# Three float32r products or one plain float32 product: the context's dense work in a two-layer hybrid backbone

## The chip, the cores and the metric

The kernel runs on one core of a Trainium2 chip as one program. The metric is the device time of one execution in microseconds. The engines are TensorE (PE, with its weight loads as PEld), VectorE (DVE), ScalarE (ACT), GpSimd (POOL) and SyncE (SP), which issues the DMAs. Each has a queue that is served in order.

## The reference

Two layers over 256 context tokens and 512 latent tokens of width 1024. In each layer: a modulated RMSNorm, one input projection, three groups of mixers (S5, gated DeltaNet "GDN", RWKV-7), one output projection with a gated residual, then a modulated RMSNorm and a squared-ReLU MLP (1024 to 4096 to 1024) with a gated residual. The context reads only itself; the latents start from the context's final states. After the first layer the context goes through its output projection and MLP; in the second layer only its states are needed, so its input projection there makes 17 blocks of 128 columns in place of 27, and no output.

```python
hc = rmsnorm(ctx, norm_mlp[layer]) * (1.0 + cmods[4]) + cmods[3]
ctx = ctx + cmods[5] * sq_relu_mlp(hc, mlp_w1[layer], mlp_w2[layer])
```

All of it is float32.

## The kernel before, in words

Activations lie feature-major: tiles of 128 features by 256 (context) or 512 (latent) tokens.

**A dense product** (`product`, L290) makes a float32 product of three float32r products: the weight's high part times the activation's high part, the weight's low part times the activation's high part, the weight's high part times the activation's low part. Their matmuls are all recorded at L296. `weight` (L265) loads 128 rows of 512 values into a staging tile `wl` (L271, 256 KB, issued by SP), casts them to the high part `wh` on ScalarE (L272) and subtracts to get the low part `wo` on VectorE or GpSimd (L273): VectorE for the context's products and the modulation, GpSimd for the latents' output projection and MLP. Each of the three tags has three buffers. `split` (L281) does the same to an activation (L284, L285), and `act_norm` (L974) to a normed one (L980, L981). One tile of weights serves four row tiles: 12 matmuls.

**The arena.** Working tiles come from 18 pages of eight units of 256 columns. A page holds plain or rounded (float32r) values; `set_rounded` (L152) converts pages, each with a copy of one column on the new page (`new_page`, L142, L147). Units are handed out in the order of emission, by a rank of when they are likely to be free. `own` lends pages to S5's pieces.

**The order.** The code emits pairs of jobs (one GDN and one RWKV job of two heads each): three pairs for the context, three for the latents, in each layer. `run_jobs` (L1257) emits each pair's preparation before the recurrences of the one before it. After certain pairs a hook emits dense work: `context` (L1206) after the context's last pair of the first layer: modulation, output projection and MLP of the context; `latents` (L1213) after the latents' last pair: the latents' output projection, then, by way of `between` in `back`, the second layer's input projection of the context (`front`), then the latents' MLP. Each piece is emitted with a class of urgency (`prio`), the recurrences first and the dense work near the end, and a scheduler lays out every engine's queue at build time from these classes. So the context's dense work is interleaved with the recurrences of the latents' pairs, and the order on each engine is fixed before the run.

In the MLP (`back`, L1129) a block of 512 hidden values is four `dense` products of eight row tiles; ScalarE takes the ReLU (L1146), VectorE squares it (L1147), `split` makes its parts, and eight products of four row tiles add to the residual (L1156). The output projection (`out_proj`, L1098) loads the mixers' outputs, splits them, and adds to the residual at L1119. Other lines that are named below: L885 is S5's gate, a plain float32 product of two row tiles of 128 x 128 for each half of the columns and each part of the tokens; L1311, L1318 and L1324 are the heads' loads and stores.

Of the kernel before, what the change touches and what calls it, by code (L numbers as in the profile page):

```python
# [11 lines left out]
AF = mybir.ActivationFunctionType  # L12
# [8 lines left out]
T = CT + LT  # L21
# [3 lines left out]
# tags of small shared tiles: columns, buffers  # L25
# [3 lines left out]
# the arena: pages of UNITS units of UNIT columns  # L29
UNIT, UNITS, PAGES = 256, 8, 18  # L30
PLAIN, ROUND, OWN = range(3)
# classes of urgency
CHAIN, LEVEL, READ, PREP, S5, DENSE, FILL = range(7)

# when the next pair of jobs is prepared, by pair: before the rest of the pair, after its first inverses, after
# its second ones, at its end
# [21 lines left out]
# the mixers' outputs in the order of the rows of the output projection: S5, then by pair of heads  # L58
Y_ORDER = (0, 1, 2, 5, 3, 6, 4, 7)
HALVES = (slice(0, 64), slice(64, 128))  # L60
# columns of a group pair's S5 constants: read-out (re, im), drive, direct part, phases
# [3 lines left out]
class Part:  # L65
    """the context or the latents: first token, tokens, modulation's column."""
# [4 lines left out]
    def chunk(self, d, n):  # L71
        """the chunk of step n in direction d."""
        return self.nc - 1 - n if d else n

    def chunks(self, d, n0, n1):
        """the chunks of the steps n0 .. n1 as a slice."""
        if d == 0:
            return slice(n0, n1)
        return slice(self.nc - 1 - n0, self.nc - n1 - 1 if n1 < self.nc else None, -1)
# [10 lines left out]
class Kern:  # L90
# [26 lines left out]
    def prio(self, c):  # L117
        """what is emitted inside is scheduled before the higher classes, in its own order."""
# [16 lines left out]
    def d(self, w):  # L135
        """a short-lived tile of the dense work."""
        return self.tile("s", w)

    # The arena hands out units by the order of emission: they go back at the end of the scope they are
    # taken in, or with release() of the list keep. Each free unit carries a rank of when it is likely to  # L140
    # be free indeed. A page holds plain float32 or float32r values.
# [10 lines left out]
    def set_rounded(self, count):  # L152
        """makes count of the pages hold float32r."""
# [13 lines left out]
    def own(self, count, late, pieces):  # L167
        """lets what the pieces emit take its tiles from count pages of its own; late: jobs that they outlast."""
# [14 lines left out]

    def s(self, w, p=P, keep=None, kind=None):
# [5 lines left out]
        for pg in self.pages:  # L190
            if pg.kind != kind:
                continue
            for o in range(0, UNITS - u + 1):
# [3 lines left out]
                # early free, not beside tiles of another life, not across quarters and halves  # L197
# [36 lines left out]
    def load_layer(self, l):  # L234
# [4 lines left out]
        # derived columns  # L239
# [25 lines left out]
    def weight(self, src, eng):  # L265
        """the parts of 128 rows of up to 512 values; eng: the engines that take turns at the low one."""
# [9 lines left out]
    def rows(self, src, eng):  # L276
        """by row tile the parts of 4 x 128 rows of a block of 128 columns."""
# [12 lines left out]
    def product(self, ps, w, acts, first=True, last=True, fresh=False):  # L290
        """ps += sum over k of w[k].T @ act[k]; fresh: the low parts of acts come last."""
        nc = self.nc
        terms = [[(hi, ah), (lo, ah), (hi, al)] for (hi, lo), (ah, al) in zip(w, acts)]
# [4 lines left out]
    def dense(self, src, acts, n, eng, fresh=False):  # L298
        """out^T[128 cols, tokens] for one block of 128 columns, in psum."""
# [6 lines left out]
    def rows_rstd(self, ps, n, scale, eps, tag):  # L306
        """(ps * scale + eps) ** -0.5 on a small token-major tile."""
# [7 lines left out]
    def bcast(self, r, w, sel, nt, tag, rt):  # L315
        """r [128 tokens, w per tile] back to feature-major, in psum; rt: scratch."""
# [18 lines left out]
    def solve(self, probs, nc_):  # L335
        """probs: pairs of blk, ytt. blk(h): [128, step, direction, 64] whose rows of half h hold strictly
        triangular blocks N on their diagonal; the inverses of I - N replace them. ytt takes the transposes
# [1582 lines left out]
```

## Time and profile before

| what | value |
|---|---|
| median of 3 timed runs | 3077.45 us (3076.12 to 3078.54) |
| span of the profiled execution, first to last instruction | 3056.7 us |
| PE busy | 2669.4 us (87%), 19956 matmul records |
| DVE, ACT, POOL busy | 1833.7, 1186.7, 1134.5 us |
| mean granted TensorE clock | 0.875 |
| DMA | 401.73 MB, 41.6% of 16 engines for the main queue |

The timed executions have no separate figure for the profiled one; its span stands 20.75 us below their median. The page counts an engine as busy from the start to the end of each instruction; matmuls are pipelined, so the distance between two starts is shorter than the time of one. In the chain that ended last the line of the dense products (L296) has 35% of the span.

### The profile page before, as it was taken

What the parts mean: (1) busy time and instruction counts of PE and PEld (TensorE: products, weight loads), DVE (VectorE), ACT (ScalarE), POOL (GpSimd) and SP (SyncE); (2) the same over time, 40 slices, a digit from 0 to 9 for tenths busy, and PEclk for the clock granted to TensorE, in tenths of its full rate; (3) what the DMA queues carried; (4) which work ended last, traced back from release to release, by engine and by line L of the source; (5) the groups of instructions that cost most, each with busy time, mean ns of one, the idle gap of its engine ahead of it and who ended that gap; (6) DMA issues with size and microseconds to landing.
All of it is one profiled execution on the core that took longest, in us unless ns stands there. A gap on an engine that the chain in (4) does not pass through costs nothing.

```text
span 3056.7 us, 54445 instructions
## 1 busy us (share of the span) xinstructions
PE 2669.4 (87%) x19956; PEld 2044.2 (67%) x19956; DVE 1833.7 (60%) x4462; ACT 1186.7 (39%) x2411; POOL 1134.5 (37%) x1274
## 2 busy tenths in 40 slices
PE   5789998865898999987899989889887889799998
PEld 1667776543566888876666768667655567477776
DVE  6654878765667756647876562647776753332223
ACT  2344445332534543445423423353334432133332
POOL 2532335424133121123446644344442522244443
PEclk9788999676787999987999999889987859699998
DMA  5345546543653543535233332255555632022222
GB/s 196 96 140 185 151 136 210 154 130 86 200 161 120 166 157 116 167 114 161 85 88 111 125 96 93 102 187 159 148 184 165 211 93 86 28 83 94 93 94 86
DMA packets 324651, 401.73 MB, mean 131 GB/s; under 512 B 142880, under 2 KB 173472, under 8 KB 324256
## 3 DMA queue, kind: packets, MB, share of 16 engines
q1 hardware_dynamic: 324384, 398.24, 41.6%
q8 instruction: 158, 2.59, 0.4%
q14 instruction: 109, 0.89, 0.1%
HBM read 300.76 MB, written 88.90 MB: 127 GB/s over the span
## 4 chain that ended last, share of the span: by engine, by line
PE 53%; DVE 19%; DMA 9%; issue 5%; ACT 4%; SPq 3%; POOL 1%; DVEq 0%; ACTq 0%; POOLq 0%
PE d L296 35%; DMA page<-dr 3%; DVE solve L371 3%; DVE solve L373 3%; PE rc L1733 2%; DVE wo L273 2%; PE rc L1732 2%; PE p L1622 1%; DVE s L472 1%; DMA dr<-page 1%; SPq L352 1%; DMA s<-s 1%; DMA wl<-in_w_dram 1%; ACT wh L272 1%; PE p L481 1%
## 5 line engine op out<-in xcount | busy, mean ns | idle before, releaser
L296 PE MATMUL d<-page,wh 128*128 128x512 f32 (+1 forms) x5024 | 1424.8, 367 | 61.0 <-DVE page L1156 15.5
L296 PEld LDWEIGHTS d<-page,wh 128*128 128x128 f32 x5024 | 919.0, 196 | 234.5 <-DVE page L1156 18.0
L296 PE MATMUL d<-page,wo 128*128 128x512 f32 (+1 forms) x2512 | 915.2, 365 | 5.5 <-DVE wo L273 4.3
L272 ACT CAST wh<-wl 128x512 fp32r<-128x512 f32 (+1 forms) x750 | 457.1, 616 | 710.2 <-PE d L296 421.0
L273 POOL TENSOR_TENSOR wo<-wl,wh 128x512 fp32r<-128x512 f32 (+1 forms) x357 | 471.8, 1325 | 672.0 <-ACT wh L272 635.8
L296 PEld LDWEIGHTS d<-page,wo 128*128 128x128 f32 x2512 | 493.4, 196 | 80.6 <-DVE wo L273 5.8
L273 DVE TENSOR_TENSOR wo<-wl,wh 128x512 fp32r<-128x512 f32 (+1 forms) x393 | 296.1, 758 | 112.6 <-ACT wh L272 104.1
L1156 DVE SCALAR_TENSOR_TENSOR page<-d,mod,page 128x512 f32<-128x512 f32 (+1 forms) x192 | 124.8, 659 | 199.6 <-PE d L296 199.1
L371 DVE TENSOR_TENSOR solve<-solve 128x30 f32<-128x30 f32 (+4 forms) x360 | 151.3, 420 | 21.6 <-issue 12.0
L1147 DVE TENSOR_TENSOR s<-s 128x512 f32<-128x512 f32 (+1 forms) x96 | 60.5, 631 | 172.1 <-ACT s L1146 172.0
L373 DVE TENSOR_TENSOR solve<-solve 128x30 f32<-128x30 f32 (+4 forms) x360 | 142.8, 397 | 7.7
L1499 POOL TENSOR_TENSOR g<-g,gates 64x128 f32<-64x128 f32 x120 | 59.5, 496 | 219.7 <-DVE g L1504 190.4
L285 DVE TENSOR_TENSOR page<-s,page 128x512 fp32r<-128x512 f32 (+1 forms) x118 | 86.6, 738 | 47.5 <-ACT page L284 47.3
L1146 ACT ACTIVATE s<-d 128x512 f32<-128x512 f32 (+1 forms) x96 | 50.6, 527 | 141.5 <-PE d L296 141.4
L472 DVE SCALAR_TENSOR_TENSOR s<-s,ncol,s 128x256 f32<-128x256 f32 (+1 forms) x132 | 96.4, 733 | 3.0
L284 ACT CAST page<-s 128x512 fp32r<-128x512 f32 (+1 forms) x118 | 64.1, 547 | 80.5 <-DVE s L1147 62.9
L926 PE MATMUL d<-wo,scp 128*2 128x512 f32 x160 | 76.3, 477 | 20.6 <-DVE wo L273 19.6
L1622 PE MATMUL p<-page,page 64*128 64x128 f32 (+1 forms) x576 | 84.7, 307 | 10.4 <-DVE page L1625 7.1
L1622 PEld LDWEIGHTS p<-page,page 64*128 64x128 f32 x576 | 73.1, 209 | 27.4 <-issue 12.8
L1733 PE MATMUL rc<-page,page 128*64 128x64 f32 x464 | 86.7, 275 | 2.8 <-DMA page<-dr 2.8
L481 PE MATMUL p<-consts,page 128*128 128x128 f32 x348 | 63.8, 309 | 25.0 <-DMA page<-dr 11.2
L1732 PE MATMUL rc<-page,r 64*64 64x64 f32 x432 | 79.2, 270 | 5.6 <-DVE r L1724 4.0
(464 smaller groups left out, 4057.7 us busy)
## 6 DMA issues: line engine op xcount, KB each, us to landing
wl<-in_w_dram SPq DMA_DIRECT2D x384, 256.0 KB, 2.6
wl<-in_mod_w_dram SPq DMA_DIRECT2D x160, 256.0 KB, 3.0
wl<-in_w_in_dram SPq DMA_DIRECT2D x142, 256.0 KB, 2.9
page<-dr SPq DMA_DIRECT2D x118, 256.0 KB, 3.3
dr<-s SPq DMA_DIRECT2D x72, 256.0 KB, 2.5
dr<-page SPq DMA_DIRECT2D x30, 512.0 KB, 4.1
dr<-page SPq DMA_DIRECT2D x55, 256.0 KB, 2.5
page<-dr SPq DMA_DIRECT2D x16, 834.0 KB, 5.2
```

The costliest lines, as they stand in the source:

```text
L272: nc.scalar.copy(hi, st)
L273: low.tensor_tensor(lo, st, hi.bitcast(F32), OP.subtract)
L285: nc.vector.tensor_tensor(lo, src, hi.bitcast(F32), OP.subtract)
L296: nc.tensor.matmul(ps, x, y, start=(first and i == 0), stop=(last and i == len(order) - 1))
L371: nc.vector.tensor_tensor(tm, y3[:, :j, j:j + 1].to_broadcast([P, j, w]), y3[:, j:j + 1, j + 1:].to_broadcast([P, j, w]), OP.mult)
L373: nc.vector.tensor_tensor(y3[:, :j, j + 1:], y3[:, :j, j + 1:], tm, OP.add)
L472: nc.vector.scalar_tensor_tensor(acc, cp[:, j:j + n], w[:, 5 * i + j:5 * i + j + 1], acc, OP.mult, OP.add)
L481: self.nc.tensor.transpose(p[:, t * 128:(t + 1) * 128], src[:, t * 128:(t + 1) * 128], self.ident)
L1156: nc.vector.scalar_tensor_tensor(x[j], ps, mod[:, 40 + j, g:g + 1], x[j], OP.mult, OP.add)
L1622: nc.tensor.matmul(ps[:, i], flat(bk[d][hs, n0 + i]), kr[d][hs, n0 + i], start=True, stop=True)
L1732: nc.tensor.matmul(o, st[hs, d], kr[d][hs, n, 1], start=True, stop=False)
L1733: nc.tensor.matmul(o, xv[h][:, n, d], self.R[d][:, h, n], start=False, stop=True)
```

## The change

The context's output projection, its MLP and its input projection of the second layer call the same helpers with no split engine (`eng` is None). `rows` then loads the weights into `wl` and hands them to the matmul as they are; the activations are plain float32 tiles too, taken from pages that `held` sets aside (three for output projection and MLP, one for the input projection). `product` makes one matmul call for each row tile. The conversion to four rounded pages ahead of the context's dense work goes away; the latents' conversion to six stays. The small second products of the decay and learning rate (`lora`) keep their splits on VectorE. The rest of the diff takes out comments.

```diff
-PLAIN, ROUND, OWN = range(3)
+PLAIN, ROUND, OWN, HELD = range(4)
...
+    @contextmanager
+    def held(self, count):
+        free = sorted((p for p in self.pages if p.kind == PLAIN and None not in p.rank), key=lambda p: max(p.rank))[:count]
+        assert len(free) == count
+        for p in free:
+            p.kind = HELD
+        yield
+        for p in free:
+            p.kind, p.rank = PLAIN, [max(max(p.rank), self.now + 0.5)] * UNITS
...
     def rows(self, src, eng):
+        if eng is None:
+            st = self.wide("wl")
+            self.nc.sync.dma_start(st, src.rearrange("p k n -> p (k n)"))
+            st = st.rearrange("p (k n) -> p k n", k=4)
+            return [st[:, k] for k in range(4)]
...
     def product(self, ps, w, acts, first=True, last=True, fresh=False):
         nc = self.nc
+        if not isinstance(w[0], tuple):
+            for i, (x, y) in enumerate(zip(w, acts)):
+                nc.tensor.matmul(ps, x, y, start=(first and i == 0), stop=(last and i == len(w) - 1))
+            return
...
-    def act_norm(self, x, part, gain, mod, sh, rs=None):
+    def act_norm(self, x, part, gain, mod, sh, rs=None, plain=False):
         nc, acts = self.nc, []
         for k, h in enumerate(self.norm(x, part, gain, mod, sh, rs)):
+            if plain:
+                t = self.s(part.n, kind=HELD)
+                nc.scalar.activation(t, h, AF.Identity, bias=mod[:, sh + k, part.g:part.g + 1])
+                acts.append(t)
+                continue
...
-        eng = 'p' if part is LAT else 'v'
+        eng = 'p' if part is LAT else None
...
-                    t = self.d(n)
+                    t = self.s(n, kind=HELD) if eng is None else self.d(n)
                     nc.sync.dma_start(t, self.yd[l, part][k])
-                    b = self.new_act(n)
-                    self.split(b, t)
+                    if eng is None:
+                        b = t
+                    else:
+                        b = self.new_act(n)
+                        self.split(b, t)
...
-                            r = self.d(n)
+                            r = self.s(n, kind=HELD) if eng is None else self.d(n)
                             nc.scalar.activation(r, ps, AF.Relu)
                             nc.vector.tensor_tensor(r, r, r, OP.mult)
+                            if eng is None:
+                                us.append(r)
+                                continue
                             b = self.new_act(n)
                             self.split(b, r)
...
         def context():
-            self.set_rounded(4)
             mods(1, 0, 2, 1, 3)
             xc[:] = self.load_x(xin(CTX), CTX, kc)
-            self.out_proj(0, CTX, xc, (0, 1))
-            self.back(0, CTX, xc, lambda: mods(0, *range(4 + 6, 12)))
+            with self.held(3):
+                self.out_proj(0, CTX, xc, (0, 1))
+                self.back(0, CTX, xc, lambda: mods(0, *range(4 + 6, 12)))
...
-            self.back(0, LAT, xl, lambda: self.front(1, ((CTX, xc, kc),), 'v'))
+            def front1():
+                with self.held(1):
+                    self.front(1, ((CTX, xc, kc),), None)
+            self.back(0, LAT, xl, front1)
```

## Rows read from the trace of the kernel before

**Rows 1.** Busy time by stretch: from:to, us; PE, PEld, DVE, ACT, POOL (instructions); clock, DMA share, GB/s.
```profile
814.00:940.00 126.00, 111.39 (x1036) 78.57 (x1035) 87.87 (x215) 51.33 (x108) 37.11 (x43) 0.78 0.50 152
940.00:1215.00 275.00, 262.27 (x3112) 229.80 (x3113) 185.78 (x457) 122.22 (x257) 53.01 (x69) 0.95 0.46 143
1215.00:1281.00 66.00, 58.64 (x441) 55.40 (x440) 53.52 (x180) 33.99 (x69) 5.76 (x5) 0.95 0.56 183
...
1325.00:1430.00 105.00, 84.94 (x564) 74.88 (x564) 66.89 (x157) 59.49 (x141) 29.65 (x55) 0.84 0.49 151
...
1470.00:1920.00 450.00, 420.01 (x2587) 324.23 (x2587) 271.33 (x603) 158.91 (x312) 231.27 (x232) 0.97 0.34 104
```

**Rows 2.** The same stretches, instructions of L296 alone: PE, PEld, clock, DMA share, GB/s.
```profile
814.00:940.00 126.00, 29.99 (x192) 26.40 (x192) 0.78 0.50 152
940.00:1215.00 275.00, 157.94 (x1120) 142.22 (x1121) 0.95 0.46 143
1215.00:1281.00 66.00, 56.52 (x425) 53.77 (x424) 0.95 0.56 183
...
1325.00:1430.00 105.00, 60.25 (x408) 56.42 (x408) 0.84 0.49 151
```

**Rows 3.** Groups by shape, 814 to 1430: count, busy us, mean ns, idle before and releasers.
```profile
L296 PE MATMUL d<-page,wh 128*128 128x256 f32 x1424 | 291.3, 298 | 16.6 <-DVE page L1156 4.1 <-DVE page L981 3.8 <-ACT page L980 3.3
...
L296 PE MATMUL d<-page,wo 128*128 128x256 f32 x712 | 210.7, 296 | 3.8 <-DVE wo L273 3.8
L273 DVE TENSOR_TENSOR wo<-wl,wh 128x512 fp32r<-128x512 f32 x196 | 140.2, 720 | 46.1 <-ACT wh L272 43.8 <-PE d L926 0.2
L272 ACT CAST wh<-wl 128x512 fp32r<-128x512 f32 x215 | 131.9, 618 | 195.1 <-PE d L296 132.6 <-DMA wl<-in_w_out_dram 17.9 <-DMA wl<-in_w_dram 15.1
```

**Rows 4.** Waits of ACT, 940 to 1281: us in total, times, longest.
```profile
ACT wh L272 <- PE d L296: 77.2, 45, 5.2
```

**Rows 5.** Waits of PE, 940 to 1281.
```profile
PE d L296 <- DVE page L981: 2.8, 1, 2.8
...
PE d L296 <- DVE page L285: 2.1, 1, 2.1
PE d L296 <- DVE wo L273: 1.4, 2, 1.1
...
PE d L296 <- ACT wh L272: 1.2, 2, 0.9
```

**Rows 6.** Busy time by stretch, columns as in rows 1: two short stretches for clock.
```profile
747.30:749.40 2.10, 2.10 (x7) 0.94 (x5) 2.10 (x3) 1.02 (x3) 0.23 (x1) 1.00 0.00 0
1242.30:1245.20 2.90, 2.90 (x27) 2.90 (x26) 2.86 (x13) 1.27 (x3) 0.00 (x0) 1.00 0.51 143
```

**Rows 7.** Timeline of PE in the context's MLP: start us, us, instruction, count.
```profile
1243.09 0.40 PE L296 MATMUL d<-page,wh 128*128 128x256 f32 x2
1243.32 0.28 PE L296 MATMUL d<-page,wo 128*128 128x256 f32 x1
1243.44 0.40 PE L296 MATMUL d<-page,wh 128*128 128x256 f32 x2
```

**Rows 8.** Timeline of PE in S5's gate.
```profile
747.28 0.59 PE L885 MATMUL d<-page,page 128*128 128x256 f32 x2
747.72 1.02 PE L885 MATMUL d<-page 128*128 128x512 f32 x2
748.58 1.02 PE L885 MATMUL d<-page,page 128*128 128x512 f32 x2
```

**Rows 9.** Line L885 in the whole trace: count, ns min/median/max, first and last start.
```profile
L885 PE MATMUL d<-page,page x24: 379/613/1220, 743.7 to 2359.9; 128*128 128x256 f32 x12, 128*128 128x512 f32 x12
...
L885 PE MATMUL d<-page x8: 379/592/667, 730.5 to 748.1; 128*128 128x256 f32 x4, 128*128 128x512 f32 x4
```

**Rows 10.** Waits of SP's queue, 940 to 1281.
```profile
SPq L271 <- DVE wo L273: 116.8, 59, 14.4
```

**Rows 11.** Weight tiles (wl), 900 to 1430, from issue to landing.
```profile
DMA to landing us min/median/max: 2.2/2.8/5.6
```

More of the change, by code (lines that the diff above doesn't have):

```diff
@@ L1000, in front @@
             for part, x, kept, *rs in parts:
-                acts.append(self.act_norm(x, part, col["norm_mix"], mod, 0, *rs))
+                acts.append(self.act_norm(x, part, col["norm_mix"], mod, 0, *rs, plain=eng is None))
                 self.release(kept)
@@ L1061, in lora @@
                         nc.vector.tensor_tensor(y[HALVES[1 - d], :n], x[hs], y[hs, :n].bitcast(F32), OP.subtract)
-                        hi, lo = self.weight(a["ups"][l, i, d], eng)
+                        hi, lo = self.weight(a["ups"][l, i, d], eng or "v")
                         for f in range(3):
@@ L1132, in back @@
         col, mod = self.par[l]
-        eng = 'p' if part is LAT else 'v'
+        eng = 'p' if part is LAT else None
         with self.prio(DENSE):
@@ L1137, in back @@
             with self.scope():
-                acts = self.act_norm(x, part, col["norm_mlp"], mod, 24)
+                acts = self.act_norm(x, part, col["norm_mlp"], mod, 24, plain=eng is None)
                 for fb in range(8):
```

## The prediction, made before any run of the changed kernel

> **What bounds the kernel now.** I read the busy time of each engine by stretch first, because the change touches three stretches only: the context's output projection (814 to 940 us, with modulation products in it), the context's MLP (940 to 1281) and the second input projection of the context (1325 to 1430). In 940 to 1281 TensorE is busy 262.27 + 58.64 = 321 of 341 us, VectorE 239, ScalarE 156 [rows 1]. The reader is to see that TensorE has 20 us left there, VectorE 102. In the first and the third stretch TensorE has 15 and 20 us left [rows 1].
>
> The same windows for the line of the dense products alone give 157.94 + 56.52 = 214 us of TensorE in 940 to 1281, so the heads' work takes 107 there; in the third stretch 60 of 85 [rows 2]. The groups by shape show what is replaced: 1424 + 712 = 2136 products of 256 columns, and beside them the splits of weights: 196 on VectorE of 0.720 us, 215 casts of 0.618 us on ScalarE (both counts hold some of other weights) [rows 3].
>
> Then the waits. ScalarE's cast of a weight stands 77.2 us, 45 times, behind TensorE [rows 4]: the high and low parts have three buffers each and TensorE has not read the old ones. TensorE in turn waits 2.8 + 2.1 + 1.4 + 1.2 = 7.5 us for splits of activations and weights [rows 5]. So weights are ready before TensorE wants them. In the context's MLP the dense work is bound by TensorE, not by what the change takes away.
>
> **The price of a product.** At the full clock (the clock column reads 1.00, the level of 2.4 GHz, for both stretches that I use [rows 6]) three split products start 1243.44 - 1243.09 = 0.35 us apart in all, 0.117 each [rows 7]. The plain product exists in this kernel too, in the gate of S5 (L885). Two of its records of 256 columns take 747.72 - 747.28 = 0.44 us, two of 512 columns 748.58 - 747.72 = 0.86 [rows 8]. So one record of 256 columns is 0.215 us, which looks like a bargain against 0.35. But the code there makes 2 layers x 2 halves x 2 parts x 2 row tiles = 16 products, and the trace holds 24 + 8 = 32 records [rows 9]. Each plain product is two records: 0.43 us against 0.35 for the three. The change makes the dense work 0.08 us dearer for each 128 rows by 256 columns: 64 products in the output projection (+5 us), 512 in the MLP (+41), 136 in the input projection (+11), 57 us in all.
>
> TensorE's weight loads are the place to weigh a rule. In 940 to 1215 they are busy 229.80 of 275 us [rows 1], yet the steps of 0.117 us [rows 7] show that they overlap. The Trainium skill (Perfetto Trace Analysis, Identifying the Most-Contended Engine) calls the busy share of matmuls a bad measure and that of LDWEIGHTS a good one. By that rule the change would relieve TensorE, since 2136 loads become 1424; by the measured starts it burdens it. I go by the starts; the other result is the last rival.
>
> **The change part by part.** The sum is made on the profiled execution (span 3056.7); the timed runs' median is 20.75 us above that span, and I add the difference in the span to the median.
>
> Output projection (814 to 940): +5 us of TensorE beside 15 idle ones [rows 1], so nothing of it need reach the end; if that cover is gone it costs the 5. Sixteen weight tiles lose their cast and split, and eight loaded outputs theirs. The heads' recurrence of the first latent pair runs through the same stretch and does not change. Bounds: nothing, and 16 x 0.720 = 11.5 us [rows 3] if every VectorE split were on the path. I take 7 gained, since the products queue behind VectorE's triangular solve as well, which stays.
>
> MLP (940 to 1281): +41 on the engine that bounds it. Back come the 7.5 us of waits for splits [rows 5]. The bare steps of 1545 records are 1545 x 0.117 = 181 us against 214 busy [rows 2]; about 10 of the 33 us between are the mean clock of 0.95 [rows 1], and of the remaining 23 (last passes and short gaps) I give back half, 12, since a square feeds the product without cast and split, and ScalarE's queue no longer stands behind TensorE. 41 - 7.5 - 12 = 21 later. Bounds: TensorE's floor, 107 + 512 x 0.43 = 327, which would be 14 earlier; and the full 41 later.
>
> Input projection (1325 to 1430): +11 of TensorE, 20 idle, 36 splits on VectorE less. This stretch also waits for transfers, shifts and convolutions. Bounds -12 (the idle time filled, the +11 paid out of it, and the start of the norm a little earlier) and +11; I take +2, near the middle.
>
> Transfers: the same count and bytes. What moves is the wait: SP's issue of a weight now stands mostly on VectorE's split (116.8 us, 59 times) [rows 10]; afterwards on TensorE's last product of the tile three before. Queued behind it on SP are the heads' loads and stores, and their recurrences wait for those. A transfer lands in 2.2 to 5.6 us, 2.8 in the middle [rows 11]; two tiles of four products, 3.44 us, cover the middle one and not the longest. I count it as nothing, as the middle says; the rival below has its price.
>
> Pages: three set aside in place of four that hold rounded values, one page more for the heads; the conversion of four pages goes away before the output projection, and at the latents six are converted in place of two. Each is a copy of one column on VectorE that waits for the page's last reader, with VectorE's queue behind it. Counted as nothing: VectorE has 102 us free. If that cover fails, a wait like the longest of an in-order engine on these products, 5.2 us [rows 4], is the bound for one, either way.
>
> What follows starts with the end of these stretches. The latents' MLP (1470 to 1920) keeps TensorE busy 420 of 450 us [rows 1] and is not edited, so a delay passes through whole. Sum: -7 + 21 + 2 = +16, so 3077.45 + 16 = **3093 us**.
>
> **Rivals.**
> - **TensorE is filled to its floor** (faster). VectorE loses some 92 us of splits in 940 to 1281 (128 tiles of 0.720 us [rows 3]); the heads' steps, which queue behind them, come sooner and leave no gaps. For it: only 107 of the 341 us are the heads' TensorE work. Against it: TensorE is at 321 of 341. The place is 940 to 1281, and it decides when over 20 of the 41 us are regained there. Its time: -14 - 12 - 12 = -38, 3039.
> - **Three buffers are too few** (slower still). A weight tile is held till TensorE is through, not till it is split, so the lead over TensorE shrinks from weights and parts, six deep, to three. It decides where a landing takes over 3.44 us. At the longest, 5.6, a tile's turn is (5.6 + 1.72) / 3 = 2.44 us, 0.72 over its 1.72; if a third of the 178 tiles land so, 59 x 0.72 = 43 more: 3136. For it: the DMA share is 0.46 to 0.56 already [rows 1], and SP serves all in order. Against it: the middle landing of 2.8 us.
> - **Nothing reaches the end**: regained waits and dearer products cancel, 3077.
> - **Weight loads bound TensorE**: 712 loads fewer at a step of 0.117 us each [rows 7] are 83 us, 2994. The starts of plain records [rows 8] speak against it, though only a few stand in a row in this trace.
>
> **How the numbers follow.** A measurement of this kernel can tell about 0.2% (6 us) from no change. Forecast case 0.46 (its own range +0 to +36: 0.39 slower, 0.07 within 6 us); floor rival 0.26, faster; three buffers 0.16, slower; nothing 0.08 (0.05 same, 0.02 faster, 0.01 slower); loads 0.04, faster. Faster 0.32, same 0.12, slower 0.56. Those on the slower side hold 0.55 with a range of their own of 3083 to 3138; the whole range, with the upper half of the floor rival in, is 3042 to 3138.
>
> **What would show it.** Right: in the context's MLP the records of the dense line number 1024 at 0.215 us and its stretch is some 20 us longer, with TensorE over 94% busy; no casts of weights there; SP's longest waits are on TensorE; the output projection's stretch a few us shorter. Wrong: one record for each product; a context MLP that ends before 1281; TensorE idle for long before the dense line, released by transfers of weights (then it is the buffers); or a first latent pair that starts elsewhere than near 814, since the order of all engines is laid out anew at build time.

## The result, and the profile after

The changed kernel takes 3149.32 us (median of 4 runs, 3146.77 to 3152.09) against 3076.78 for the kernel before beside it: a ratio of 1.0253, 95% interval 1.0223 to 1.0283. It is slower by 72 us where the prediction had 16. The profiled execution took 3152.09 us, its span is 3150.1.

In the changed kernel the plain products are recorded at L312, the split ones at L317 (L296 before); plain weight tiles are issued at L291 and split ones at L282 (L271 before), L1175 and L1188 are the ReLU and the residual's sum (L1146, L1156 before).

Busy time by stretch of the changed kernel, columns as in [rows 1]: output projection, MLP, second input projection.

```profile
830.00:955.00 125.00, 111.52 (x1047) 77.39 (x1047) 78.08 (x201) 41.77 (x91) 41.08 (x49) 0.82 0.46 136
955.00:1330.00 375.00, 362.04 (x3036) 285.15 (x3036) 135.17 (x361) 69.92 (x160) 47.16 (x67) 0.96 0.44 137
1375.00:1490.00 115.00, 96.45 (x433) 76.03 (x434) 45.33 (x121) 43.62 (x111) 27.13 (x56) 0.83 0.49 151
```

The same stretches for L312 alone, columns as in [rows 2].

```profile
830.00:955.00 125.00, 33.97 (x128) 24.96 (x128) 0.82 0.46 136
955.00:1330.00 375.00, 242.76 (x1024) 190.64 (x1024) 0.96 0.44 137
1375.00:1490.00 115.00, 71.41 (x272) 56.55 (x272) 0.83 0.49 151
```

The count settles the price's first half: 128 + 1024 + 272 = 1424 records for 712 products, two each. Beside [rows 1], the MLP's stretch grew from 341 to 375 us, TensorE in it from 321 to 362, while VectorE fell from 239 to 135 and ScalarE from 156 to 70. TensorE has 13 us left where it had 20.

The timeline of PE there shows the other half, as [rows 7] did for the split steps: 13 records from 1199.69 to the next instruction at 1202.59, 0.223 us each, 0.45 a product. The third line has the busy time of that stretch, columns as in [rows 1]; its clock column reads 1.00, as it did for the two prices of the prediction.

```profile
1199.69 2.97 PE L312 MATMUL d<-page,wl 128*128 128x256 f32 x13
1202.59 0.45 PE L1548 MATMUL gc<-page,g 128*64 128x64 f32 x8
...
1199.70:1202.50 2.80, 2.80 (x14) 2.28 (x12) 1.48 (x4) 0.38 (x1) 0.00 (x0) 1.00 0.03 7
```

Waits in 955 to 1330 of PE and SP, and the landing of weight tiles in 900 to 1490 (columns as in [rows 5], [rows 10] and [rows 11]).

```profile
PE d L312 <- DMA wl<-in_w_dram: 4.1, 5, 2.0
...
SPq L291 <- PE d L312: 211.2, 106, 7.0
...
DMA to landing us min/median/max: 2.4/2.7/6.4
```

TensorE's waits for splits [rows 5] are gone, and 4.1 us of waits for transfers have come. SP waits on TensorE as foretold, 211 us in all, and by these rows it hardly matters: a weight is late five times. Whether more staging tiles would gain anything, e3 below has to tell.

A row of SP gives the length of a piece between its first and its last weight transfer, which I use from here on where nothing else is said. The first line is the context's MLP of the kernel before (profile on which the prediction rests), the second that of the changed kernel, the third the changed kernel's second input projection (columns: count; min/median/max ns; first and last start).

```profile
L271 SPq DMA_DIRECT2D wl<-in_w_dram x128: 327/328/1350, 915.0 to 1272.0; - x128
```

```profile
L291 SPq DMA_DIRECT2D wl<-in_w_dram x128: 327/328/1191, 931.1 to 1323.6; - x128
...
L291 SPq DMA_DIRECT2D wl<-in_w_in_dram x34: 327/330/859, 1362.3 to 1475.2; - x34
```

The MLP went from 357.0 to 392.5 us, the projection from 102 to 113. This length has a weakness: the first transfer goes out ahead of the first product, and not by the same time in every kernel. The products of the MLP themselves, in the kernel before, in the changed one and in e4 (an experiment below):

```profile
L296 PE MATMUL d<-page,wh x1024: 276/279/681, 943.7 to 1279.0; 128*128 128x256 f32 x171
```

```profile
L312 PE MATMUL d<-page,wl x1024: 379/379/796, 968.2 to 1328.4; 128*128 128x256 f32 x171
```

```profile
L301 PE MATMUL d<-page,wl x1024: 379/379/795, 937.4 to 1312.7; 128*128 128x256 f32 x171
```

From the first to the last of them it is 335 us before, 360 in the change and 375 in e4: 25 and 40 us more, where the transfers say 36 for both. So the size of the MLP's part depends on the measure, by up to 15 us between the two kernels.

The rest of the 72 us lies outside the three parts. Transfers of weights read from SP's queue (the first of a piece where nothing else is said), and the end of the span, in us (e0 is the kernel before run again; e4, e13 and e15 are experiments below):

| | output projection | MLP of the context | latents' MLP, 10th tile | latents' MLP, last | second layer's MLP | end |
|---|---|---|---|---|---|---|
| before, e0 | 823 | 925 | 1483 | 1918 | 2657 | 3062 |
| changed | 830 | 931 | 1553 | 1987 | 2747 | 3150 |
| e4 | 817 | 915 | 1507 | 1946 | 2690 | 3094 |
| e13 | 824 | 921 | 1527 | 1959 | 2689 | 3094 |
| e15 | 822 | 923 | 1505 | 1944 | 2688 | 3092 |

The output projection starts 7 us late in the changed kernel, before a plain product has run; the latents' MLP gets going late; and the second layer, where nothing was edited, loses another 20 us.

### The profile page after: what moved, and what is told of

It reads as the page before. It is cut to its first block, busy times and chain, and to the rows that moved or that the text cites. A ratio compares the mean times of both kernels' runs of the same rounds, so it can differ in the third digit from the quotient of the medians.

```text
span 3150.1 us, 52340 instructions
## 1 busy us (share of the span) xinstructions
PE 2755.5 (87%) x19244; PEld 2058.0 (65%) x19244; DVE 1713.9 (54%) x4227; ACT 1070.4 (34%) x2193; POOL 1134.2 (36%) x1275
## 5 line engine op out<-in xcount | busy, mean ns | idle before, releaser
L317 PE MATMUL d<-page,wh 128*128 128x512 f32 (+1 forms) x3600 | 1133.1, 394 | 46.3 <-DVE page L1188 12.8
L317 PEld LDWEIGHTS d<-page,wh 128*128 128x128 f32 x3600 | 683.0, 195 | 206.2 <-DVE page L1188 16.0
L317 PE MATMUL d<-page,wo 128*128 128x512 f32 (+1 forms) x1800 | 705.6, 392 | 3.3 <-POOL wo L284 3.0
L283 ACT CAST wh<-wl 128x512 fp32r<-128x512 f32 (+1 forms) x572 | 348.1, 616 | 608.4 <-PE d L317 329.5
L317 PEld LDWEIGHTS d<-page,wo 128*128 128x128 f32 x1800 | 351.1, 195 | 74.5 <-POOL wo L284 5.9
L312 PE MATMUL d<-page,wl 128*128 128x256 f32 x1424 | 348.1, 398 | 9.0 <-DMA wl<-in_w_dram 4.1
L312 PEld LDWEIGHTS d<-page,wl 128*128 128x128 f32 x1424 | 272.2, 197 | 59.0 <-issue 6.0
L1188 DVE SCALAR_TENSOR_TENSOR page<-d,mod,page 128x512 f32<-128x512 f32 (+1 forms) x192 | 125.3, 660 | 257.8 <-PE d L317 172.9
L284 DVE TENSOR_TENSOR wo<-wl,wh 128x512 fp32r<-128x512 f32 (+1 forms) x214 | 166.7, 790 | 108.7 <-ACT wh L283 98.4
L301 DVE TENSOR_TENSOR page<-s,page 128x512 fp32r<-128x512 f32 x78 | 71.7, 921 | 45.8 <-ACT page L300 45.6
L946 PE MATMUL d<-wh,scp 128*4 128x512 f32 x160 | 80.4, 503 | 12.9 <-ACT wh L283 10.8
```

The lines of the kernel that those rows point to most:

```text
L283: nc.scalar.copy(hi, st)
L284: low.tensor_tensor(lo, st, hi.bitcast(F32), OP.subtract)
L312: nc.tensor.matmul(ps, x, y, start=(first and i == 0), stop=(last and i == len(w) - 1))
L317: nc.tensor.matmul(ps, x, y, start=(first and i == 0), stop=(last and i == len(order) - 1))
L946: nc.tensor.matmul(ps[:4], self.scp[:, k], hi, start=(k == 0), stop=False)
L1188: nc.vector.scalar_tensor_tensor(x[j], ps, mod[:, 40 + j, g:g + 1], x[j], OP.mult, OP.add)
```

## The experiments

Three theories. **Price**: two records for three steps, and little regained. **Buffers**: three staging tiles are too few. **Pages and order**: other pages, and an order laid out anew at build time, delay work that the change doesn't edit. Ratios are to the kernel before in the same batch; its medians there were 3060 to 3063 us.

### Each part alone, and more staging tiles

e0 is the kernel before again. e1 has only the projection plain, e2 only output projection and MLP:

```diff
# e1: out_proj, back; the context keeps set_rounded(4)
-        eng = 'p' if part is LAT else None
+        eng = 'p' if part is LAT else 'v'
# e2: latents
-                with self.held(1):
-                    self.front(1, ((CTX, xc, kc),), None)
+                self.front(1, ((CTX, xc, kc),), 'v')
# e3: in held, three more staging tiles in the pages set aside
+        mine = []
+        self.turn6, self.extra = 0, [self.s(512, keep=mine, kind=HELD) for _ in range(3)]
...
-            st = self.wide("wl")
+            self.turn6 += 1
+            st = self.wide("wl") if self.turn6 % 2 else self.extra[self.turn6 // 2 % 3]
...
-            with self.held(3):
+            with self.held(4):
...
-                with self.held(1):
+                with self.held(2):
```

> The kernel before once more, for a second profile beside the first, whose span (3056.7 us) stands 20 us below the median of the timed runs. If the 24 us by which the changed kernel's unedited stretches are longer than in the first profile are the spread between executions, this profile shows most of them too (span 3070 to 3077). If they come from the change (the order on the engines, laid out anew), its unedited stretches agree with the first profile within 2 us each.

> Plain products in the context's second input projection alone, the rest as before. The theory of the price (two records of 0.215 us in place of three steps of 0.117, 136 products, little regained) says +8 to +15 us on the kernel before. The theory of the new order (the layout costs, wherever it is touched) says up to +30. The theory of the buffers (three staging tiles held till TensorE is through) says more than the price, since this stretch has the most other transfers: +15 to +25.

> Plain products in the context's output projection and MLP alone, the second input projection with splits as before. Price: 576 products, +46 us at most, some 8 regained: +35 to +45. Buffers: the same here, and it must fall with more staging tiles. Order: with the projection alone the two differ from the full change by more than 15 us in sum.

> The changed kernel with six staging tiles for the plain weights in place of three (three more from one more page set aside). Price: within 8 us of the changed kernel, because SP's wait on TensorE only moves. Buffers: 20 us or more come back, and TensorE's waits for transfers of weights in the context's MLP (4.1 us in sum by the profile) and the gaps before its dense products vanish.

e0: 0.9998 (0.9971 to 1.0025). e1: 3153.74 us, 1.0301 (1.0267 to 1.0335): the cheapest part alone, 136 products, costs as much as the whole change, though its own stretch grows by 7 to 8 us (1313 to 1423) and the last tile of the latents' MLP is issued at 1920, as in e0 (1918). e2: 3126.97, 1.0209 (1.0172 to 1.0246). The parts don't add up, so the price is not all of it. e3: 3183.93, 1.0393 (1.0362 to 1.0424), slower than the change. From its first to its last weight transfer its MLP is no shorter than with three staging tiles:

```profile
L295 SPq DMA_DIRECT2D page<-in_w_dram x64: 327/328/916, 872.3 to 1268.3; - x64
```

That is 396.0 us against 392.5. But with six tiles the first transfers go out earlier, so this length can't tell here, and e3 sets other pages aside than the change. The kernel to hold it against is e11 (below), with the same numbers of pages set aside and three staging tiles. The plain products of output projection and MLP, from e3 (two of its groups), then from e11:

```profile
L316 PE MATMUL d<-page,wl x576: 379/379/796, 834.4 to 1278.3; 128*128 128x256 f32 x192
L316 PE MATMUL d<-page,page x480: 379/379/793, 838.0 to 1280.5; 128*128 128x256 f32 x160
```

```profile
L312 PE MATMUL d<-page,wl x1152: 379/379/796, 834.7 to 1300.0; 128*128 128x256 f32 x192
```

They take 446 us in e3 and 465 in e11 (469 to 471 in e12, e15 and e16, which set four pages aside too and have three staging tiles). For the same two pieces, from the first product of the output projection to the last of the MLP, the kernel before takes 447 (832.1 to 1279.0) and the change 488 (840.8 to 1328.4). So in this stretch six staging tiles are worth some 19 us. At the end little of it is left: e3 at 1.0393 and e11 at 1.0430 are not told apart, since their intervals overlap. Buffers are not the 72 us, but that they cost nothing isn't shown. In e1 and e3 a new thing appears: the preparation of pair 9 (the second layer's first latent pair) is cut in two with over 200 us between, and its triangular solution starts at 2318 and 2339 in place of 2108.

### The price, with the pages of the kernel before

```diff
# e4 on the kernel before (e5: the same in front alone)
+        if eng is None:
...
+            return [st[:, k] for k in range(4)]
...
+                nc.tensor.matmul(ps, x, y.bitcast(F32), start=(first and i == 0), stop=(last and i == len(w) - 1))
...
+            if plain:
+                nc.scalar.activation(hi, h, AF.Identity, bias=shift)
+                acts.append((hi, lo))
+                continue
...
```

> All three parts as plain products, as in the change, but with the pages of the kernel before: every activation keeps its pair of float32r units, takes the value in the high one (rounded to it, so the low parts of these activations are left out of the result), and the plain product reads that unit as float32; the weights stay in their staging tile. What a page holds when is then what it was before, while the order of each engine is again laid out at build time. Price alone (two records of 0.215 us for three of 0.117): the context's MLP, 357 us from its first to its last weight transfer before, takes 357 + 41 - 7 = 391, the second input projection 103 + 5 to 10, and nothing else changes: 3063 + 40 to 50 = 3103 to 3113 us, and the last MLP's first weight transfer at 2657 + 45 = about 2700. Pages (the pages moved by the change cost some 35 to 40 of its 72 us): the same numbers, so the whole time falls from 3149 to 3103 to 3113. Order (the sequence laid out at build time, and not the pages, delays the last pairs): 3140 or more although the context's part comes out at +45, with pair 9's solution after 2200 instead of at 2110.

> Only the second input projection plain, as in the earlier run that took 3154 us, but with its activations in the pairs of units of the kernel before (high part alone, so the low parts of its activations are left out). Pages: the preparation of pair 9 isn't cut in two, the last MLP's first weight transfer stays near 2657, and the whole is 3063 + 0 to 10 = 3063 to 3073 us. Order: 3130 or more, with pair 9's solution again near 2300.

e4: 3099.68, 1.0123 (1.0099 to 1.0146). e5: 3070.96, 1.0038 (1.0018 to 1.0057). In the pages of before the change costs 38 us, not 72 to 77, and the projection 9.5, not 91. e4's MLP:

```profile
L281 SPq DMA_DIRECT2D wl<-in_w_dram x128: 327/328/753, 915.2 to 1307.9; - x128
```

392.7 us, as in the changed kernel and 36 more than before; its output projection takes 98 us to the MLP's start where the kernel before takes 101, its input projection 107 (1346.6 to 1453.6) where the kernel before takes 102. The end is 32 us behind e0 in the two profiles, after a start 5 us ahead: here the context's delay passes through, as I had counted (e13 and e15 will show that it need not).

### Relief and price apart

```diff
# e6 on the kernel before, weights of the three parts
...
+            self.nc.scalar.copy(hi, st)
+            hi = hi.rearrange("p (k n) -> p k n", k=4)
+            return [(hi[:, k], hi[:, k]) for k in range(4)]
# e7 on the changed kernel
+            hi, lo = self.wide("wh", F32R), self.wide("wo", F32R)
+            self.nc.scalar.copy(hi, st)
+            self.nc.vector.tensor_tensor(lo, st, hi.bitcast(F32), OP.subtract)
# e10 on the kernel before, in out_proj, back and front
-        eng = 'p' if part is LAT else 'v'
+        eng = 'p' if part is LAT else 'vp'
```

> The kernel before with its three split steps, but for the weights of the three parts VectorE's subtraction is left out and the high part stands in for the low one (so the low parts of these weights are left out of the result): VectorE's relief without the price, in the pages of before. My prediction gave the MLP 7.5 to 12 us for it: 357 - 12 = 345 us between its first and last weight transfer. If the relief is worth what the change's own stretch shows (41 of price, 34 lost): 350. If nothing waits for VectorE: 357. The whole between 3045 and 3063 us, if the order laid out anew moves nothing.

> The changed kernel, but the casts and subtractions of the weights are still made, into tiles that nothing reads: the price without the relief, in the pages of the change. If the relief is worth 7 us in the MLP: 393 + 7 = 400 us between its first and last weight transfer and 3149 + 10 = 3159. If nothing waited for VectorE and ScalarE once TensorE is slower: 393 and 3149. If the relief was worth more than I read (12 and 7.5, both taken): 393 + 20 = 413 and 3169 or more.

> The kernel before, exact, with the low parts of these three parts' weights taken in turns by VectorE (0.69 us each) and GpSimd (1.30 us each, busy for 65 of the 357 us of the context's MLP): half of the relief without the price of plain products. If the relief is what bound the kernel there: half of the 32 us that leaving out all these subtractions gave, 3061 - 16 = 3045 us, MLP at about 349. If GpSimd's longer subtraction holds TensorE as VectorE's did: 3061 and 357 or slightly longer.

e6: 3029.80, 0.9899 (0.9873 to 0.9926). e7: 3138.13, 1.0252 (1.0221 to 1.0283), the change's own ratio. The MLP of e6, then of e7:

```profile
L279 SPq DMA_DIRECT2D wl<-in_w_dram x128: 327/328/1306, 923.6 to 1263.9; - x128
```

```profile
L291 SPq DMA_DIRECT2D wl<-in_w_dram x128: 327/328/1936, 930.7 to 1312.7; - x128
```

With split products, VectorE's relief takes the MLP from 354 to 357 down to 340, and the whole down by 32. That the whole falls is clear of the spread; where is less sure, since from first to last product e6's MLP takes 324 us, and e8 (below), which makes every subtraction, 325. With plain products the relief is worth nothing that shows: e7 makes every cast and subtraction, its MLP is at 382.0 no longer than without, and its input projection at 118.7 is 6 us longer. Its engines there, columns as in [rows 1], with VectorE at 228 us:

```profile
931.00:1313.00 382.00, 358.55 (x3051) 283.37 (x3050) 228.01 (x507) 149.85 (x301) 63.45 (x77) 0.96 0.42 137
```

The two effects are not a sum. e10: 3067.44, 1.0008 (0.9982 to 1.0033), MLP 932.8 to 1292.4: no gain from half of the relief; the last section has what stands against it.

### Which pages

e8 and e9 take other float32r pages in the kernel before (three; the second to the fifth). The others vary the pages of kernels with plain products:

```diff
# e8 (e9: gone = free[1:5] there)
         def context():
-            self.set_rounded(4)
+            self.set_rounded(3)
# e13 on the changed kernel (e15: with held(4) too; e14: e4 with the projection's activations of the change)
-            if plain:
+            if plain and sh == 0:
+                t = self.new_act(part.n)
+                nc.scalar.activation(t[0], h, AF.Identity, bias=mod[:, sh + k, part.g:part.g + 1])
...
+                y = y[0].bitcast(F32) if isinstance(y, list) else y
# e16 on the changed kernel (e12: the first edit alone; e11: held(4) and held(2))
-            with self.held(3):
+            with self.held(4):
...
-                t = self.s(part.n, kind=HELD)
+                t = self.s(part.n, kind=HELD if sh else None)
...
-                with self.held(1):
-                    self.front(1, ((CTX, xc, kc),), None)
+                self.front(1, ((CTX, xc, kc),), None)
# e17 on the changed kernel, in held
+        free = free[3:4] if count == 1 else free[:count]
```

> The kernel before with three instead of four float32r pages for the context's output projection and MLP: the same instructions but for the marking of a page, the same prices, other pages for the tiles around, and an order laid out anew. Pages/order: it moves the time by tens of us although no work changes, up or down; the place is where a milestone first leaves the kernel before by over 10 us while the lengths of the context's MLP (357 us) and of the second input projection (103 us) stay within 5. If pages and order are harmless, as the prediction counted them: 3061 within 10 us, each milestone within 10.

> The kernel before with four float32r pages for the context as before, but the second to the fifth of the free ones in the order of their ranks instead of the first to the fourth: nothing else differs in the program's text. Pages/order: over 15 us away from 3061, either way. Harmless: 3051 to 3071 us.

> The changed kernel with four and two pages set aside instead of three and one, as in the run with six staging tiles, but with the three staging tiles of the change. If the staging tiles cost nothing there and all of that run's difference was its pages: the same as it, 3180 within 15 us, with the context's MLP again starting near 872 and lasting about 396 us. If the staging tiles mattered: the MLP lasts some 10 us longer than its 396, or starts later. If the change's own choice of three and one is as good as any: 3149.

> The changed kernel with four pages set aside for the context instead of three, one for the second input projection as in the change. If three pages are the cause of the late start of the latents' MLP (10th weight transfer at 1553 in the change, 1502 with four and two pages): about 1505 there. Whether the last pairs follow isn't given by that: 3100 to 3115 if pair 9's preparation runs in one piece, 3180 to 3200 if it is cut in two as with four and two.

> The changed kernel, but the second input projection's plain products read the high units of float32r pairs, as in e4 (the low parts of these activations left out): only the context's three pages are those of the change. If these three carry the cost: as the change, 3140 to 3155. If the projection's page does: as e4, 3100. Both in part, as the run with the output projection and MLP alone has it (3127, without the projection's price of about 5): 3130.

> As e4 (all plain, output projection and MLP in the pages of the kernel before, high parts alone), but the second input projection's activations in one page set aside, as in the change. If that page cuts pair 9's preparation in two whatever stands before it: 3100 + 80 to 90 = 3180 to 3190 with pair 9's solution 200 us later than the preparation's start. If the cut was chance of one layout: 3100 to 3120.

> The changed kernel with four pages set aside for the context, the same four that the kernel before makes float32r, and the projection's activations in the high units of float32r pairs: plain products at the price alone. If the choice of pages is all that the change loses beyond the price: 3100 to 3110 us, as e4. If the six pages that the latents then have to mark anew cost something: 3115 or more, from the latents' MLP on.

> The changed kernel, exact, with four pages set aside for the context's output projection and MLP and none for the second input projection, whose activations take any free float32 units. By the allocation as the kernel is built, no tile of pair 9's preparation falls on a page of the second layer's S5. Page mechanism: pair 9's preparation runs in one piece, and the time is that of the price alone, 3095 to 3115 us. If plain products in exact float32 pages cost more than the price for another reason: 3140 or more.

> The changed kernel, but the one page set aside for the second input projection is the fourth of the free ones in the order of their ranks instead of the first. By the allocation as the kernel is built, a tile of four units of pair 9's RWKV preparation then falls on a page of the second layer's S5, which it doesn't in the change. Page mechanism: pair 9's preparation is cut in two, its solution comes after 2300 us, and the time is 3175 to 3200 us against the change's 3149. If the allocation foretells nothing: 3149 within 10.

e8: 3075.26, 1.0033 (1.0014 to 1.0051), a little slower, by nothing but pages and the order that goes with them. e9: 3070.47, 1.0018 (0.9995 to 1.0041), not told apart from no change. With everything plain, us, by what the projection's activations lie in (rows) and the pages of the context's output projection and MLP (columns):

| | four float32r | three set aside | four set aside |
|---|---|---|---|
| float32r units | 3100 (e4) | 3099 (e13) | 3099 (e15) |
| free units, none set aside | | | 3098 (e16, no low parts left out) |
| one page, the first free | 3188 (e14) | 3149 (the change) | 3180 (e12) |
| one page, the fourth free | | 3205 (e17) | |
| two pages | | | 3196 (e11) |

(The change ran beside a kernel before of 3077 us, the others beside 3060 to 3063; by its ratio it would stand at 3139 here. The ratios of e11 to e15 are 1.0430, 1.0388, 1.0130, 1.0416 and 1.0124, each good to 0.5% or better.) The context's pages make no difference to the whole while the projection's activations lie in float32r units, three medians within 1 us; with four set aside, the projection's page costs 3180 - 3098 = 82. For e13 I had 3130 as the middle case; the three pages carry nothing by themselves. Yet e2, the same three pages with a split projection, is 36 us above what e4 leaves without the projection's price (3127 against 3100 - 9.5), so pages don't add up either.

The first row holds a second lesson. The MLPs of e4, e13 and e15 take 393, 395 and 382 us, and e13 issues the 10th weight tile of the latents' MLP some 21 us after e15 (table above). By the second layer's MLP the three are within 2 us of each other, and they end alike. So a later context isn't always a later end; what makes up for it in the second layer, these runs don't show.

Why one page costs so much can be followed. `own` gives S5 of the second layer the five free pages of the lowest ranks; a page set aside for the projection displaces the tiles that lay there, S5 gets other pages, and then nothing early is free for a tile of pair 9's RWKV preparation (`xv`, the values by step). Printed while the kernels are built, e17's allocation has this line (time of emission, page, units, rank), and the change's has none of rank 20.6 for that pair:

```
now 17.50 page 11 u 4 rank 20.60 prep:1637
```

Rank 20.6 is that of S5's pages. Of the kernels here, e1, e3, e11, e12, e14 and e17 have such a line: 3154, 3184, 3196, 3180, 3188 and 3205 us. None of the others has one. e16 and e17 were foretold from it and came out at 3097.58 (1.0110, 1.0072 to 1.0148) and 3204.95 (1.0461, 1.0420 to 1.0501), the second 5 us over the range that I had given it.

The trace shows it happen. The four copies into the two `xv` tiles of pair 9 on ScalarE, in e16 and then in e17 (columns as for SP above; under e17's what ended the idle time before them):

```profile
L1631 ACT COPY page<-p x4: 364/368/370, 2095.7 to 2096.9; 64x256 f32<-64x256 f32 x4
```

```profile
L1633 ACT COPY page<-p x4: 365/368/370, 2121.1 to 2339.3; 64x256 f32<-64x256 f32 x4
...
  PE d L907: 0.6, 1
```

e17's timeline of ACT and POOL: L907 and L908 are S5's gate (L885 in the kernel before and the line behind it), L910 its last step.

```profile
2337.86 0.47 ACT L908 ACTIVATE page<-d,ncol 128x256 f32<-128x256 f32 x1 [0.18 <-PE d L907]
2338.90 0.76 ACT L1633 COPY page<-p 64x256 f32<-64x256 f32 x2 [0.56 <-PE d L907]
```

```profile
2338.76 2.14 POOL L910 TENSOR_SCALAR page<-page 128x768 f32<-128x768 f32 x1 [5.67 <-DVE page L909]
2340.87 1.93 POOL L1634 TENSOR_SCALAR page<-page 64x512 f32<-64x512 f32 x1
```

The second tile's copies stand from 2121 to 2338 behind the products of S5's gate. In the other five kernels with such a line the same copies lie 214 to 226 us apart, and under 3 us in all kernels without one. The products of that preparation (L1658 in e16, L1660 in e17) show the cut: PE busy, clock, DMA share, GB/s, in four stretches.

```profile
2080.00:2130.00 50.00, 1.42 (x8) 0.93 0.49 156
2130.00:2150.00 20.00, 3.47 (x24) 1.00 0.40 134
2150.00:2340.00 190.00, 0.00 (x0) 0.82 0.47 155
2340.00:2360.00 20.00, 5.21 (x32) 0.83 0.65 197
```

So pair 9's solution, whose first step on VectorE is at 2139.7 in e16, comes at 2371.2 in e17:

```profile
L394 DVE TENSOR_TENSOR solve<-solve x60: 190/358/1801, 2139.7 to 2385.7; 128x30 f32<-128x30 f32 x4, 128x58 f32<-128x58 f32 x4, 128x84 f32<-128x84 f32 x4, 128x108 f32<-128x108 f32 x4
```

```profile
L395 DVE TENSOR_TENSOR solve<-solve x30: 190/386/1408, 2371.2 to 2439.1; 128x30 f32<-128x30 f32 x2, 128x58 f32<-128x58 f32 x2, 128x84 f32<-128x84 f32 x2, 128x108 f32<-128x108 f32 x2
```

How much of e17's 107 us is this wait, and how much the clock that goes with it, isn't separated: the mean granted clock is 0.857 in e17 and 0.876 in e16, and in 2350 to 2600 it is 0.64 and 0.74, with TensorE busy for 194 and 220 of the 250 us.

In the changed kernel itself pair 9's preparation runs in one piece (solution at 2184), and its page costs some 38 us against e13 by the ratios in another way, spread over the run. By the two profiles: 9 by the end of the projection, 26 by the 10th weight tile of the latents' MLP, 40 by the end of the second layer's input projection, 58 by its MLP. These two profiles come from different batches, whose kernels before differ by 17 us, and their mean granted clocks are 0.870 and 0.879, so they show where time is lost rather than how much. No single wait holds it, and how much is the page, how much the order laid out with it and how much the clock stays open. No kernel here that leaves nothing out beats the one before; of those with plain products in all three parts e16 is the fastest.

## Why the prediction was wrong

**The bound, and the price of a product: right.** TensorE bounds the context's MLP, a plain product is two records, and the price fell where it was put. The rival of the weight loads falls: 512 loads fewer in the MLP, and its products take 25 to 40 us longer. The rival of the three buffers had 43 us on top of the forecast; weights are late by 4.1 us in all, and six staging tiles shorten output projection and MLP by 19 us (e3 against e11) without a faster end that can be told from none. So it isn't the cause of the 72 us; the transfers, which I counted as nothing, hold some 19 us of that stretch. The ratio of e4 means 38 us for the whole price where the sum had 16.

**The MLP's term was mis-sized.** I took 41 - 7.5 - 12 = 21. It measured 392.7 - 357.0 = 36 in e4 and the same in the change by the transfers, so 5 to 6 us came back of 19.5; by the products it is 40 in e4 and 25 in the change. Over all the kernels here the plain MLP takes 379 to 396 us by the transfers and the split one 352 to 360, so this size is good to some 10 us. The step that failed is giving back what VectorE and ScalarE no longer do as if it stood beside the price. That relief exists (e6: 32 us in all, 14 to 17 in the MLP by the transfers), but only while split products need the splits; with plain products even the full load of idle casts and subtractions costs nothing that shows (e7).

**The two smaller terms**: output projection -3 in e4 for my -7; input projection 107 for 102 us, +5 for my +2 (the splits that this term counts as 36 are 34, one for each weight transfer; the sum doesn't use them). With the MLP's 15 these make up the 22 us between 16 and 38.

**Pages counted as nothing: wrong, and by the largest amount.** The change's ratio less e4's is 1.30%, 40 us. My bound of 5.2 us was the longest wait of an in-order engine on a matmul; the wait that a page can make is that of a tile for a reader in another job, 217 us in e17. The changed kernel has no such wait: that its 40 us come with the projection's page is shown by e13, by what steps is not. VectorE's 102 us of free time, which I named as the cover, are no cover for a tile that must not be written yet.

**A delay passes through whole**: it does in e4 against e0, and it doesn't in e13 against e15, where 21 us at the latents' MLP are gone by the second layer's. So this step was a guess that e4 bears out and not a rule. The start of the first latent pair was named as the sign of a moved order; the output projection that runs beside it started 7 us later than in e0, but a rerun of the kernel before moves by as much (814 and 823), so this sign was too weak to read.

## What to carry to other kernels

Price a replaced product by the records that the trace has for one product, and give back a neighbour's freed time only if an experiment with the new bound in place shows it: two kernels, one with the relief alone and one with the price and idle work, tell it. Where tiles are placed at build time, a change of placement is an edit like any other: print the allocation, look for tiles that land on a page whose reader is a whole job away, and run the new instructions in the old places before the time is put down to the instructions. Where two kernels differ in buffers, compare stretches from product to product: a first transfer that goes out earlier makes a stretch look longer.

## What the runs showed of the hardware beyond that

Halving VectorE's subtractions (e10) freed only 249 - 240 = 9 us of VectorE's busy time between the MLP's first and last weight transfer, not 64 x 0.71 = 45, and other VectorE work got slower while GpSimd took the other half. The split of an activation, and GpSimd's low parts, in e0 and then in e10 (groups by shape, columns as in [rows 3]):

```profile
L273 DVE TENSOR_TENSOR wo<-wl,wh 128x512 fp32r<-128x512 f32 x128 | 90.7, 711 | 20.1 <-ACT wh L272 18.2
L1156 DVE SCALAR_TENSOR_TENSOR page<-d,mod,page 128x256 f32<-128x256 f32 x60 | 28.2, 480 | 19.4 <-PE d L296 19.1
...
L285 DVE TENSOR_TENSOR page<-s,page 128x256 fp32r<-128x256 f32 x32 | 13.3, 417 | 0.7 <-ACT page L284 0.7
```

```profile
L285 DVE TENSOR_TENSOR page<-s,page 128x256 fp32r<-128x256 f32 x32 | 29.7, 928 | 11.6 <-ACT page L284 11.6
L1156 DVE SCALAR_TENSOR_TENSOR page<-d,mod,page 128x256 f32<-128x256 f32 x60 | 28.2, 480 | 18.7 <-PE d L296 18.3
...
L273 POOL TENSOR_TENSOR wo<-wl,wh 128x512 fp32r<-128x512 f32 x63 | 83.9, 1332 | 133.1 <-ACT wh L272 110.1 <-issue 11.3 <-PE gc L1488 8.5
```

The split's mean went from 417 to 928 ns, while the sum that takes one operand from psum (L1156) stayed at 480. The mean mixes two kinds, as the line's own row in e10 shows (ns min/median/max):

```profile
L285 DVE TENSOR_TENSOR page<-s,page x32: 408/1204/1310, 978.3 to 1284.0; 128x256 fp32r<-128x256 f32 x32
```

The seven splits beside which GpSimd ran nothing took 408 to 425 ns. One that began while GpSimd made a low part ended 0.28 us after it, in e10's timeline of POOL and DVE:

```profile
1084.31 1.27 POOL L273 TENSOR_TENSOR wo<-wl,wh 128x512 fp32r<-128x512 f32 x1 [2.87 <-ACT wh L272]
1084.65 1.21 DVE L285 TENSOR_TENSOR page<-s,page 128x256 fp32r<-128x256 f32 x1 [0.47 <-ACT page L284]
```

The Trainium skill (GPSIMD Engine Reference, Specifications) says that GpSimd's way to memory is shared with VectorE, and that VectorE's instructions with two inputs from SBUF contend with it; these rows agree.
